# One hybrid encoder layer: the instruction order of the whole program taken from the scheduler's timeline model

## The chip, the cores and the metric

The kernel runs on one core of a Trainium2 chip. The core has five engines that work side by side, each through its own queue in order: TensorE (PE, matrix products and transposes by a product with the identity), VectorE (DVE), ScalarE (ACT), GpSimd (POOL) and SyncE (SP), which here does nothing but issue DMA transfers. An instruction that has to wait for another engine holds up everything behind it on its own engine. The metric is the time of one execution on the device in microseconds (us); less is better.

## The reference

One layer is applied with the same weights to two sequences, 1024 tokens (`x_prompt`) and 256 tokens (`x_sample`), 1280 rows of width 1024 in all, in float32. Cut to what matters:

```python
h = rmsnorm(x); p = h @ w_in                      # one projection, columns shared out
# group A: gated DeltaNet, 4 heads of 128, both directions
qkv = silu(conv5(p[qkv_a])); q, k = l2norm(q), l2norm(k)
#   chunked delta rule per direction: a triangular solve in each chunk, then a scan over the chunks
#   v_new = u - w @ S;  o = q_dec @ S + A @ v_new;  S = S * exp(g) + k_end^T @ v_new
o_a = rmsnorm_head(o_forward + o_backward) * silu(z)
# group B: attention, 4 query heads and 2 key/value heads of 128, RMS-normalised, rotary positions
o_b = softmax(q k^T / sqrt(128)) v
x = x + rmsnorm(concat(o_a, o_b) @ w_out)
x = x + rmsnorm(square(relu(rmsnorm(x) @ w_up)) @ w_down)   # width 4096
```

## The kernel before, in words

Products that need more than one pass's precision are made of three float32r products: each operand is split into a high part (a cast on ACT, L79) and a low part (a subtraction on DVE or POOL, L80), and hi·hi, hi·lo and lo·hi are summed in one PSUM tile. The helper `split` has therefore one pair of lines for almost every stage, and the tile's name tells which one is meant.

The program has these stages. The times behind them are where their instructions stand in the profile of before.

- Rows are loaded, normalised and transposed (`x_proc`), and the `z` columns are projected (`nat_z`): 0 to 95 us.
- The mixed stage, 95 to 536 us. Its pieces are Python generators: `gdn_qk` and `gdn_v` project one head's columns (`proj_T`, matmuls L367 to L369 into `pt`, copied by ACT at L370), run the convolution (`conv_proj`: ACT L440, three DVE steps L443, POOL L444, ACT L445, DVE L446) and hand the result back to PE, which transposes it (`kt` L459, `qt` L473, `vt` L502). `gdn_e`, `gdn_sub` and `gdn_lev` make the decay matrices (`pe` L516 and L522, `pk` L528, `C` L531) and the triangular inverse; `att_proj` projects and rotates the attention heads (`prk` L423). A string written out by hand, `ORDER`, says in which order the generators are stepped. There are 12 convolutions, so 12 such hand-overs from DVE back to PE.
- The scan and attention, 536 to 791 us. `step` (L795 to L842) does one chunk of one head and both directions: products `p` on PE (L798, L800), `r` on DVE (L805), `p` on PE (L810), `vt` on ACT (L813), `p` on PE (L817, L826), then the next state on DVE (L823). The eight chunks of the prompt follow one another, four heads side by side. All calls of `step` are recorded ahead of the attention groups' second half (`att_PV`); scores (`att_S`: `ps_s` L712 to L714, maximum L715 on DVE, exponential L721 on ACT, scaling L727 on POOL) are asked for some 15 tiles ahead (`LA`).
- Output projection and norms (`out_prep`, `out_mm`, `out_norm`, `to_M`): 762 to 938 us.
- The MLP's first product (`up_w`, `up_mm` L1145 to L1147, `up_post`), in a scheme with seven products in place of eight: 906 to 1333 us; its second product (`down_prep`, `prod` L1283 to L1285, sums into `acc` on DVE): 1333 to 1672 us; a last slice with the final norm: 1672 to 1739 us. `down_prep` loads its rows from DRAM (`fr`, L1251) where the first product had put them, and casts them on ACT (L1265).

What sets the order of instructions: Python only records them, in program order, with their tiles. When the `tile.TileContext` of `kernel` closes (L1490), its scheduler plays the recorded program through a model of the machine, in model time. Whenever an engine of the model can take an instruction, it gets, of those whose inputs and tile buffers are there by model time, the one recorded earliest. The order in which each engine got its instructions is the order of its queue on the chip, for SP's DMA issues too, and the choice of buffer among a tag's `bufs` falls in the same play. Then semaphores are put in. So program order is a rank and not the order itself: an instruction recorded later passes one that isn't ready in model time. On the chip, an engine can no longer pass anything.

The default model of the machine and the timeline model differ in how they price instructions, transfers and an engine's queue. Both are part of the library. The kernel's own code, its products, tiles, buffer counts and `ORDER` are the same under either.

## Time and profile before

| | |
|---|---|
| median of 3 runs | 1739.7 us (1735.0 to 1739.98) |
| profiled execution | 1741.06 us, of which 1739.3 us from the first instruction to the last |
| mean granted TensorE clock | 0.981 |
| DMA | 252.68 MB, mean 145 GB/s |

A page of the profile lists the busy time of each engine, then the span in 40 slices of 43.5 us, then groups of instructions. "Busy" on PE counts a matmul from start to its modelled end, and neighbours overlap: in a full stream, matmuls of 512 columns are recorded at 0.39 us each but start 0.23 us apart. "Idle before" is the time an engine stood still just before an instruction, and the name behind it is the engine, tile and line whose end let it go on.

### The profile page before, as it was taken

What the parts mean: (1) busy time and instruction counts of PE and PEld (TensorE: products, weight loads), DVE (VectorE), ACT (ScalarE), POOL (GpSimd) and SP (SyncE); (2) the same over time, 40 slices, a digit from 0 to 9 for tenths busy, and PEclk for the clock granted to TensorE, in tenths of its full rate; (3) what the DMA queues carried; (4) which work ended last, traced back from release to release, by engine and by line L of the source; (5) the groups of instructions that cost most, each with busy time, mean ns of one, the idle gap of its engine ahead of it and who ended that gap; (6) DMA issues with size and microseconds to landing.
All of it is one profiled execution on the core that took longest, in us unless ns stands there. A gap on an engine that the chain in (4) does not pass through costs nothing. (4 is left out here: it accounts for less than half of the span.)

```text
span 1739.3 us, 27944 instructions
## 1 busy us (share of the span) xinstructions
PE 1626.4 (94%) x9799; PEld 1387.8 (80%) x9799; DVE 1267.9 (73%) x2549; ACT 854.6 (49%) x1937; POOL 735.8 (42%) x658
## 2 busy tenths in 40 slices
PE   6999898898997999889988999999989999999997
PEld 5777776777775888668878999999888888888885
DVE  7546798996744778885759954545787978888777
ACT  5236566554345767674446644544465333333422
POOL 3212231321113334440102555554636777788763
PEclk9999999999998999999999999999999999999999
DMA  6113334445447866244333543444556544444234
GB/s 208 70 42 109 97 108 129 137 133 154 133 143 231 273 203 194 79 161 166 104 127 127 178 147 125 151 135 134 187 193 220 154 140 146 132 143 142 86 115 155
DMA packets 208779, 252.68 MB, mean 145 GB/s; under 512 B 35073, under 2 KB 163391, under 8 KB 208639
## 3 DMA queue, kind: packets, MB, share of 16 engines
q1 hardware_dynamic: 208495, 250.77, 45.9%
q8 instruction: 77, 1.26, 0.3%
q14 instruction: 63, 0.52, 0.1%
q0 software_dynamic: 144, 0.13, 0.0%
HBM read 159.75 MB, written 91.10 MB: 144 GB/s over the span
## 5 line engine op out<-in xcount | busy, mean ns | idle before, releaser
L1146 PE MATMUL pd<-mh,ulo 128*128 128x320 f32 x892 | 279.6, 314 | 12.9 <-DVE ulo L80 12.8
L1145 PE MATMUL pd<-mh,uhi 128*128 128x320 f32 x892 | 276.6, 311 | 5.5 <-ACT uhi L79 5.5
L1147 PE MATMUL pd<-ml,uhi 128*128 128x320 f32 x892 | 276.9, 311 | 0.0
L1289 DVE TENSOR_TENSOR acc<-acc,pd 128x512 f32<-128x512 f32 x330 | 206.7, 678 | 44.1 <-PE pd L1285 44.1
L1283 PE MATMUL pd<-dhi,fhi 128*128 128x512 f32 x490 | 192.2, 392 | 1.0 <-DVE acc L1291 1.0
L1284 PE MATMUL pd<-dl,fhi 128*128 128x512 f32 x490 | 192.3, 393 | 0.0
L1285 PE MATMUL pd<-dhi,flo 128*128 128x512 f32 x490 | 191.9, 392 | 0.0
L1146 PEld LDWEIGHTS pd<-mh,ulo 128*128 128x128 f32 x892 | 169.1, 190 | 17.8 <-DVE ulo L80 17.8
L367 PE MATMUL pt<-h_hi,whi 128*128 128x512 f32 (+1 forms) x480 | 178.5, 372 | 0.0
L369 PE MATMUL pt<-h_hi,wlo 128*128 128x512 f32 (+1 forms) x480 | 178.4, 372 | 0.0
L368 PE MATMUL pt<-h_lo,whi 128*128 128x512 f32 (+1 forms) x480 | 178.4, 372 | 0.0
L1145 PEld LDWEIGHTS pd<-mh,uhi 128*128 128x128 f32 x892 | 168.9, 190 | 7.0 <-ACT uhi L79 7.0
L1147 PEld LDWEIGHTS pd<-ml,uhi 128*128 128x128 f32 x892 | 169.0, 190 | 0.0
L1265 ACT CAST fhi<-fr 128x1280 fp32r<-128x1280 f32 x49 | 62.1, 1267 | 212.6 <-PE pd L1284 116.2
L80 POOL TENSOR_TENSOR dl<-dw,dhi 128x1024 fp32r<-128x1024 f32 x49 | 129.0, 2633 | 43.4 <-ACT dhi L79 42.8
L1190 POOL TENSOR_TENSOR s<-u,u 128x320 f32<-128x320 f32 x32 | 34.3, 1071 | 207.6 <-ACT u L1155 140.7
L727 POOL TENSOR_TENSOR P<-P,sm 128x512 f32<-128x512 f32 (+1 forms) x72 | 73.5, 1040 | 95.3 <-DVE sm L725 39.0
L1283 PEld LDWEIGHTS pd<-dhi,fhi 128*128 128x128 f32 x490 | 92.0, 188 | 22.4 <-DVE acc L1291 1.4
L1285 PEld LDWEIGHTS pd<-dhi,flo 128*128 128x128 f32 x490 | 92.0, 188 | 20.7
L1284 PEld LDWEIGHTS pd<-dl,fhi 128*128 128x128 f32 x490 | 92.0, 188 | 20.3
L80 DVE TENSOR_TENSOR ulo<-us,uhi 128x512 fp32r<-128x512 f32 x88 | 76.3, 869 | 43.4 <-ACT uhi L79 42.5
L367 PEld LDWEIGHTS pt<-h_hi,whi 128*128 128x128 f32 x480 | 92.7, 193 | 13.5
(358 smaller groups left out, 4091.0 us busy)
## 6 DMA issues: line engine op xcount, KB each, us to landing
fr<-r_d SPq DMA_DIRECT2D x49, 640.0 KB, 4.3
vis<-vis_d SPq DMA_DIRECT2D x64, 384.0 KB, 4.2
uraw<-in_w_up SPq DMA_DIRECT2D x22, 1024.0 KB, 5.4
r_d<-s SPq DMA_DIRECT2D x128, 160.0 KB, 1.8
r_d<-u SPq DMA_DIRECT2D x96, 160.0 KB, 2.1
dw<-in_w_down SPq DMA_DIRECT2D x28, 512.0 KB, 4.9
wraw<-in_w_in SPq DMA_DIRECT2D x48, 256.0 KB, 3.7
x<-in_x_prompt SPq DMA_DIRECT2D x16, 512.0 KB, 3.4
```

What stands on the lines that cost most here:

```text
L80: (V if leng is None else leng).tensor_tensor(lo, src, f32(hi), ALU.subtract)
L367: T.matmul(pm[:, :n], lhsT=whi, rhs=h_hi[:, k, t0:t0 + n], start=(k == 0), stop=False)
L368: T.matmul(pm[:, :n], lhsT=whi, rhs=h_lo[:, k, t0:t0 + n], start=False, stop=False)
L369: T.matmul(pm[:, :n], lhsT=wlo, rhs=h_hi[:, k, t0:t0 + n], start=False, stop=(k == KD - 1))
L727: G.tensor_tensor(x[:, :kw], x[:, :kw], sm[:, 0:1].to_broadcast([128, kw]), ALU.mult)
L1145: T.matmul(pm, lhsT=w[0][:, k], rhs=mh[b, i][:, k], start=(k == 0), stop=False)
L1146: T.matmul(pm, lhsT=w[1][:, k], rhs=mh[b, i][:, k], start=False, stop=False)
L1147: T.matmul(pm, lhsT=w[0][:, k], rhs=ml[b, i][:, k], start=False, stop=(k == 3))
L1283: T.matmul(pm, lhsT=r[0][:, k, tk], rhs=w[0][:, k], start=(k == 0), stop=False)
L1284: T.matmul(pm, lhsT=r[0][:, k, tk], rhs=w[1][:, k], start=False, stop=False)
L1285: T.matmul(pm, lhsT=r[1][:, k, tk], rhs=w[0][:, k], start=False, stop=(k == Q - 1))
L1289: V.tensor_tensor(half(t, d), half(t, d), pm, ALU.add)
```

## The change

One argument of the context is added; nothing else in the file differs. The play at the close of the context uses the timeline model for the whole program, so the order of every engine's queue, the DMA issues on SP's queue and the buffers chosen can differ. The instructions themselves, their number, shapes and engines stay.

```diff
-    with tile.TileContext(nc) as tc, ExitStack() as ctx:
+    with tile.TileContext(nc, schedule_with_timeline_sim=True) as tc, ExitStack() as ctx:
         build(ctx, tc, I, O)
```

## The prediction

> **What bounds the kernel now.** I read the page's busy times first, then its slices, then a table of busy time by stage, then the waits of PE.
>
> ```profile
> PE 1626.4 (94%) x9799; PEld 1387.8 (80%) x9799; DVE 1267.9 (73%) x2549; ACT 854.6 (49%) x1937; POOL 735.8 (42%) x658
> ...
> PEclk9999999999998999999999999999999999999999
> ```
>
> PE is the bound by a wide margin: 1626.4 of 1739.3 us. An order of instructions takes no work away, so what it can win is PE's idle time, 112.9 us, and what it can lose is more of it. The stages say where that idle time lies (start and end of each stretch; its length; then for each engine busy us and count; granted clock, DMA share, GB/s):
>
> ```profile
> 0.00:95.00 95.00, 80.61 (x380) 61.45 (x381) 56.27 (x154) 35.61 (x65) 25.73 (x32) 0.98 0.40 130
> 95.00:217.00 122.00, 110.25 (x562) 90.17 (x560) 76.33 (x162) 66.32 (x188) 26.15 (x35) 0.96 0.31 86
> 217.00:391.00 174.00, 157.35 (x1306) 125.53 (x1305) 160.86 (x350) 106.66 (x282) 48.94 (x117) 0.98 0.47 126
> 391.00:536.00 145.00, 127.50 (x1152) 102.78 (x1151) 86.71 (x239) 56.31 (x178) 24.84 (x48) 0.93 0.50 147
> 536.00:741.00 205.00, 191.36 (x1225) 159.79 (x1224) 162.85 (x503) 141.54 (x430) 85.74 (x108) 0.99 0.61 197
> 741.00:791.00 50.00, 45.69 (x222) 33.71 (x223) 39.17 (x74) 34.51 (x71) 17.53 (x16) 0.97 0.43 148
> 791.00:906.00 115.00, 113.32 (x549) 94.47 (x548) 70.12 (x146) 49.78 (x112) 7.86 (x6) 1.00 0.40 135
> 906.00:1000.00 94.00, 83.48 (x534) 79.02 (x533) 91.46 (x143) 61.65 (x118) 35.42 (x24) 0.98 0.47 152
> 1000.00:1218.00 218.00, 218.00 (x1490) 218.00 (x1489) 109.67 (x187) 108.40 (x221) 113.40 (x108) 1.00 0.42 138
> 1218.00:1348.00 130.00, 119.08 (x746) 113.57 (x746) 100.30 (x141) 69.52 (x133) 72.62 (x51) 0.97 0.61 200
> 1348.00:1672.00 324.00, 324.00 (x1410) 264.44 (x1409) 269.07 (x371) 106.87 (x97) 245.55 (x93) 1.00 0.44 136
> 1672.00:1739.30 67.30, 55.75 (x241) 44.85 (x239) 45.04 (x85) 17.43 (x50) 32.06 (x26) 0.94 0.39 127
> ```
>
> Length less PE's busy time gives, stage by stage, 14.4, 11.8, 16.7, 17.5, 13.6, 4.3, 1.7, 10.5, 0, 10.9, 0 and 11.6 us. The reader is to see three things. From 1000 to 1218 and from 1348 to 1672 us, 542 us in all, PE is busy all the time: no order can be better there. In the mixed stage (95 to 536 us) PE loses 45.9 us. From 217 to 391 us (160.9 of 174) and from 906 to 1000 us (91.5 of 94) DVE is as full as PE, so there an order can only say which of the two waits.
>
> **What cannot be won.** The first matmul waits for the first rows, and after the last one the final norm must still run:
>
> ```profile
> 9.93 1.33 PE L171 MATMUL xt<-ident,xn 128*128 128x128 f32 x5 [9.93 <-DVE xn L184]
> ...
> 1727.35 0.40 PE L1454 MATMUL pd<-lwt,lrow 128*128 128x512 f32 x1
> ```
>
> 9.93 at the start and 1739.30 − 1727.75 = 11.55 at the end are chains of dependent work. 112.9 − 9.9 − 11.6 = 91.4 us is the most that an order could win.
>
> **The change part by part.** It removes and adds no instruction. It moves any of them, SP's DMA issues included, within what the dependences allow. The trace of before doesn't show the new order, so its cost has to be bounded from both sides. In the two full stretches I cost it at nothing: PE has work in hand there all the time, and DVE (109.7 of 218, 269.1 of 324) and POOL (113.4, 245.6) still have room behind it. That cover would go if a DMA load or a weight split were issued a whole step later; nothing in the rows says so. The same holds for 791 to 906 us.
>
> The mixed stage is where the order is dense. Its PE waits:
>
> ```profile
> PE pe L516 <- DVE C L531: 7.6, 6, 2.5
> PE vt L502 <- DVE vT L446: 7.2, 3, 2.6
> PE ps_s L712 <- ACT q_hi L79: 6.1, 1, 6.1
> PE prk L423 <- DVE araw L426: 4.5, 2, 3.1
> PE qt L473 <- DVE qk L446: 3.6, 2, 2.2
> PE pk L528 <- DVE prod L560: 2.3, 1, 2.3
> PE kt L459 <- DVE qk L446: 1.8, 1, 1.8
> ```
>
> (total us, times, longest.) A convolution ends on DVE at L446, and PE's transposes follow. There are 12 such hand-overs, and PE stands before 6 of them: (7.2 + 3.6 + 1.8) / 6 = 2.1 us each. At the other six, the result is there before PE reaches the transposes: the default order has slack there. One such wait, on PE and on DVE:
>
> ```profile
> 276.76 0.40 PE L369 MATMUL pt<-h_hi,wlo 128*128 128x512 f32 x1
> 276.99 0.40 PE L367 MATMUL pt<-h_hi,whi 128*128 128x512 f32 x1
> 280.04 0.66 PE L502 MATMUL vt<-ident,vT 128*128 128x128 f32 x4 [2.65 <-DVE vT L446]
> ...
> 280.80 0.63 PE L369 MATMUL pt<-h_hi,wlo 128*128 128x512 f32 x1
> 281.23 0.63 PE L367 MATMUL pt<-h_hi,whi 128*128 128x512 f32 x1
> ```
> ```profile
> 273.15 2.36 DVE L88 TENSOR_SCALAR xq<-ssq 128x20 f32<-128x20 f32 x1 [0.94 <-ACT gj L376]
> 275.54 0.18 DVE L89 TENSOR_SCALAR ngh<-xq 128x20 f32<-128x20 f32 x1
> ...
> 278.49 1.49 DVE L446 SCALAR_TENSOR_TENSOR vT<-vT,cy 128x1282 f32<-128x1282 f32 x1
> ```
> ```profile
> 272.38 2.97 POOL L444 TENSOR_TENSOR cy<-cy,vT 128x1282 f32<-128x1282 f32 x1 [8.76 <-DVE cy L443]
> ```
>
> The queue of PE holds the transposes in the middle of a projection whose other matmuls could have run; it can't pass them on the chip. They were late because a DVE instruction of 20 elements took 2.36 us where its neighbour of the same size took 0.18: it ended (275.51) with POOL's large one (275.35). Afterwards matmuls start 0.43 us apart, not 0.23.
>
> My step is this. An order dealt from a finer account of time sets each transpose where its input is due, and no later; lateness that the account doesn't see, like the 2.2 us above, then meets PE at all 12 hand-overs and not at 6. The added waits are 6 × 2.1 = 12.6 us. The slow matmuls after a wait add to that: the half-speed spell begins at or before 280.80 and is over by 284.85, when the 0.39 us records come back:
>
> ```profile
> 284.85 0.39 PE L369 MATMUL pt<-h_hi,wlo 128*128 128x512 f32 x1
> 285.08 0.40 PE L367 MATMUL pt<-h_hi,whi 128*128 128x512 f32 x1
> ```
>
> Taken as some 3.7 us, that is 3.7 × (1 − 0.23/0.43) = 1.7 us lost, an estimate. The mean clock of this stretch is 0.98 and not lower, so I charge it to half of the six waits: 5.1 us. The bounds: zero, if the added hand-overs keep their slack; and 12 × 2.6 + 12 × 1.7 = 52 us, if all 12 are hit once more by the longest wait. I take 17.7, nearest to the rows of the mean wait.
>
> [...]
>
> All other stages at zero, the sum against the profiled execution is 1741.06 + 17.7 = 1758.8. That execution lies 1.4 us above the median of before, and its span 1.8 below itself; against the median I forecast **1757 us**.
>
> **The rivals.**
>
> *Faster: the waits go.* If the timeline model is closer to the chip where it counts, PE's transposes are set behind work that really is ready. The seven rows above sum to 33.1 us, the attention's start (6.1) is a change of stage and stays; half of the other 27.0 is 13.5. From 1218 to 1348 us PE's idle 10.9 has a similar cause, an engine's queue held up by its first instruction:
>
> ```profile
> ACT fhi L1265 <- DMA fr<-r_d: 11.4, 3, 5.1
> ...
> PE pd L1146 <- DVE ulo L80: 7.5, 8, 2.6
> ```
>
> ACT stands before a cast whose rows are still on their way, while the high part of PE's next weights (L79), on which `ulo` hangs, waits behind it. Half of it is 5.5. With three half-speed spells fewer (5.1) that makes 24.1: 1716 us. For it speaks that so many waits are of the kind that a better-dealt queue avoids; against it, that DVE is full in half of the mixed stage.
>
> *Much slower: the scan loses its precedence.* The scan's chunks follow one another; each needs three visits to PE, one to DVE, one to ACT, and now finds the engines at once because it is recorded ahead of the attention. If the timeline model's engines take a queue of ready work ahead of time, a scan instruction comes in behind that. The scan's last work and the attention's:
>
> ```profile
> L856 DVE SCALAR_TENSOR_TENSOR zt<-oa,ro,zt x40: 333/343/1128, 609.7 to 740.0; 128x128 f32<-128x128 f32 x40
> ...
> L741 PE MATMUL po<-p_hi,v_lo x72: 278/394/485, 562.0 to 790.9; 128*128 128x512 f32 x64, 128*128 128x256 f32 x8
> ...
> L721 ACT ACTIVATE P<-ps_s,mx,rsa 128x512 f32<-128x512 f32 x50 | 38.7, 781 | 12.1 <-DVE mx L718 12.1
> L715 DVE TENSOR_REDUCE mx<-ps_s 128x1 f32<-128x512 f32 x52 | 35.2, 684 | 8.1 <-PE ps_s L714 7.6
> ```
>
> The scan has 790.9 − 740.0 = 51 us in hand. One attention job ahead of it at each visit costs 0.78 + 0.68 + 3 × 0.23 = 2.16 us a chunk, 17.2 over eight chunks. From three jobs deep on (52 us) the slack is gone; six deep give 104 − 51 = 53 us, and with the 17.7 above about 1810 us. For it: such a delay hits every chunk. Against it: nothing in the trace of before shows the depth.
>
> *No difference.* The waits come from late results and not from the order, or the order hardly changes: within 5 us, 1740. [...]
>
> **How the numbers follow.** Forecast (slower, some 8 to 50 us) 0.35; scan delayed (1810) 0.17; faster (1716) 0.31; no difference 0.17. About 0.3% (5 us) is what a measurement of this kernel tells from no change. So slower 0.52, faster 0.31, same 0.17. The likeliest case's own range is 1748 to 1790, from the bounds of its step. For 8 in 10 the range reaches from 1710, which leaves out the third of the fast case in which more than the priced waits go, to 1830, which leaves out a third of the scan's case.
>
> **What would show it.** Right: PE's idle time in the mixed stage goes from 45.9 to some 60 us, with more `kt`, `qt` and `vt` rows among PE's waits, more slices below full clock, and the two full stretches unchanged in length (218 and 324 us for the same counts). The scan's case: the last `oa` work later than the last `po` matmul, and a longer stretch between 536 and 906 us. The fast case: fewer PE waits on DVE before 536 us, and the `fhi` row gone from the waits of ACT. The forecast would be wrong if the full stretches lengthen, say because a POOL or DMA step was put late, or if PE's matmuls themselves take longer.

## The result and the profile after

| | before | after |
|---|---|---|
| median of 4 runs | 1739.84 us (1735.0 to 1743.97) | 1796.57 us (1795.58 to 1804.92) |
| profiled execution, its span | 1741.06, 1739.3 | 1804.92, 1803.2 |
| mean granted TensorE clock | 0.981 | 0.952 |

After stands to before as 1.0338, with a 95% interval of 1.0297 to 1.0378: 57 us slower by the medians. The prediction had the direction and, with 1710 to 1830, the range; its forecast of 1757 was 40 us short. The profiled execution of after is the slowest of its four, 8.4 us above the median; what is read from it below is tested by the experiments.

The page of after, its busy times and its clock:

```profile
PE 1637.7 (91%) x9799; PEld 1415.5 (79%) x9799; DVE 1268.6 (70%) x2549; ACT 858.3 (48%) x1937; POOL 733.2 (41%) x658
...
PEclk9999999998888999886999999999999899999999
```

The instructions are the same in number and, on DVE, ACT and POOL, in busy time. PE is busy 11 us longer, at a lower granted clock (0.952 and not 0.981), and the rest of the 64 us is idle time. A slice is 45.1 us here. The clock's row dips in slices 10 to 13 (406 to 586 us), 17 to 19 (721 to 857 us) and 32 (1398 to 1443 us). Two tables of stretches, before and then after, cut at the first attention score, the scan's end, the first transpose of the out-projection and the first matmul of the up-projection (start and end; length; busy us and count of PE, PEld, DVE, ACT, POOL; clock; DMA share; GB/s):

```profile
95.00:536.00 441.00, 395.09 (x3016) 318.47 (x3015) 323.90 (x749) 229.29 (x645) 99.92 (x199) 0.96 0.44 122
536.00:740.00 204.00, 191.16 (x1225) 159.79 (x1224) 161.85 (x500) 141.18 (x430) 85.74 (x108) 0.99 0.61 197
740.00:762.00 22.00, 17.75 (x76) 12.32 (x76) 17.19 (x35) 18.32 (x37) 9.22 (x8) 0.92 0.73 269
762.00:909.00 147.00, 143.73 (x711) 117.82 (x710) 95.47 (x195) 68.82 (x153) 16.17 (x14) 1.00 0.36 118
```
```profile
95.00:540.00 445.00, 398.08 (x3044) 329.37 (x3042) 330.52 (x753) 228.83 (x646) 94.24 (x199) 0.93 0.42 119
540.00:818.00 278.00, 234.79 (x1410) 200.29 (x1408) 188.18 (x564) 169.51 (x490) 99.60 (x124) 0.91 0.49 159
818.00:836.00 18.00, 0.00 (x0) 0.00 (x0) 9.99 (x11) 8.36 (x8) 0.00 (x0) 0.50 0.82 321
836.00:964.70 128.70, 126.26 (x601) 104.69 (x601) 74.61 (x156) 54.39 (x121) 8.45 (x6) 0.98 0.33 111
```

The mixed stage, where the prediction put its loss, idles 46.9 us after 45.9. PE's waits in it are others, though. The longest of after (total us, times, longest):

```profile
PE pe L516 <- DVE C L531: 13.1, 6, 8.3
PE pk L528 <- DVE C L531: 7.8, 4, 4.1
PE pt L367 <- ACT cp L370: 4.2, 2, 3.9
```

None of the 16 rows of this view names L446: the three rows of before that do (7.2, 3.6 and 1.8 us, six waits) are gone.

From the first score to the up-projection PE's idle time goes from 12.8 + 4.3 + 3.3 = 20.4 to 43.2 + 18.0 + 2.4 = 63.6 us, and its busy time from 352.6 to 361.1: 51.7 us in one stage. Cuts inside it show where (after):

```profile
640.00:740.00 100.00, 95.61 (x624) 82.82 (x624) 75.85 (x219) 68.23 (x186) 38.43 (x46) 1.00 0.40 128
740.00:811.00 71.00, 45.39 (x240) 38.51 (x238) 34.01 (x142) 28.18 (x104) 11.88 (x28) 0.81 0.51 171
811.00:836.00 25.00, 0.00 (x0) 0.00 (x0) 13.95 (x31) 10.74 (x18) 0.29 (x1) 0.50 0.59 231
```

Until 740 us PE is about as full as before (95.6 of 100 us). Then it is left with a third of the scan and nothing beside it, and at last with nothing at all. The groups by line say the same (shortest, median and longest ns; first and last start). `vt`, once in each step of the scan, before and after; then, of after, the last attention product:

```profile
L813 ACT ACTIVATE vt<-p,sca x80: 348/367/397, 541.6 to 727.8; 128x128 f32<-128x128 f32 x80
```
```profile
L813 ACT ACTIVATE vt<-p,sca x80: 347/366/452, 552.7 to 808.6; 128x128 f32<-128x128 f32 x80
...
L741 PE MATMUL po<-p_hi,v_lo x72: 278/394/403, 569.3 to 733.6; 128*128 128x512 f32 x64, 128*128 128x256 f32 x8
```

80 records are 40 steps of two directions. The pace of the scan falls from (727.8 − 541.6) / 40 = 4.65 to (808.6 − 552.7) / 40 = 6.40 us a step, while attention's last product comes 57 us earlier (733.6 against 790.9). Before, 44 of the 72 products stand ahead of the scan's last `vt` and 28 behind it; after, all 72 do. A stretch of the timeline of after shows how a step is made longer (start, us, engine, line):

```profile
660.79 0.63 ACT L813 ACTIVATE vt<-p,sca 128x128 f32<-128x128 f32 x2
...
661.41 0.39 PE L740 MATMUL po<-p_lo,v_hi 128*128 128x512 f32 x1
...
661.63 0.39 PE L741 MATMUL po<-p_hi,v_lo 128*128 128x512 f32 x1
...
661.86 0.60 PE L735 MATMUL ptr<-ident,P 128*128 128x128 f32 x4
...
662.22 0.36 PE L712 MATMUL ps_s<-k_hi,q_hi 128*128 128x256 f32 x1
...
662.66 0.61 PE L817 MATMUL p<-vt,vis 128*128 128x128 f32 x4
```

`vt` is there at 661.42. The scan's next product stands in PE's queue behind two attention products, four transposes and three score matmuls, all of them ready, and starts 1.24 us later with PE never idle. No row of waits shows this: PE waits for nothing, the scan waits for PE. Averaged over the 144 products that read a `vt`, the delay from the end of their step's second `vt` to their start is 0.88 us before and 1.73 after; over the 64 that read an `r`, from its end, 0.55 and 1.35.

What the scan's end is worth is seen in the queue behind it: first SP's transfers, then rows of all engines.

```profile
820.68 3.79 SPq L877 DMA_DIRECT2D wo_raw<-in_w_out  x8
```
```profile
816.36 2.19 DVE L856 SCALAR_TENSOR_TENSOR zt<-oa,ro,zt 128x128 f32<-128x128 f32 x8
...
834.00 1.04 ACT L79 CAST wo_hi<-wo_raw 128x1024 fp32r<-128x1024 f32 x1 [0.96 <-DMA wo_raw<-in_w_out]
836.05 1.09 PE L897 MATMUL otr<-ident,og 128*128 128x128 f32 x4 [26.10 <-DMA og<-og_d]
```

The out-projection needs the scan's result back from DRAM. Its weights are asked for when `zt` is done, too: 818.6 to 836.1 us is a chain of transfers and casts. Before, the same chain ran from 740 to 762 us, but PE had 17.75 us of work there, from the rest of attention.

The second place is the change from up to down. First of before (DVE, then PE), then POOL, DVE and PE of after:

```profile
1343.48 6.07 DVE L1291 COPY acc<-pd 128x512 f32<-128x512 f32 x10 [6.88 <-DMA r_d<-s]
```
```profile
1344.83 0.50 PE L1283 MATMUL pd<-dhi,fhi 128*128 128x512 f32 x1 [1.00 <-DVE acc L1291]
```
```profile
1389.87 3.59 POOL L1237 TENSOR_TENSOR dw<-dw 128x1024 f32<-128x1024 f32 x1 [6.45 <-DMA dw<-in_w_down]
1393.42 0.86 POOL L1190 TENSOR_TENSOR s<-u,u 128x320 f32<-128x320 f32 x1
1394.25 0.87 POOL L1192 TENSOR_TENSOR s<-u,u 128x320 f32<-128x320 f32 x1
1395.08 2.34 POOL L1238 TENSOR_TENSOR dw<-dw 128x1024 f32<-128x1024 f32 x1
1397.38 0.85 POOL L1191 TENSOR_TENSOR s<-s,u 128x320 f32<-128x320 f32 x1
1398.20 2.87 POOL L1267 TENSOR_TENSOR flo<-fr,fhi 128x1280 fp32r<-128x1280 f32 x1
1401.03 2.33 POOL L80 TENSOR_TENSOR dl<-dw,dhi 128x1024 fp32r<-128x1024 f32 x1
1403.33 2.33 POOL L1240 TENSOR_TENSOR dw<-dw 128x1024 f32<-128x1024 f32 x1
1405.62 0.85 POOL L1201 TENSOR_TENSOR s<-s,u 128x320 f32<-128x320 f32 x1
```
```profile
1408.54 6.07 DVE L1291 COPY acc<-pd 128x512 f32<-128x512 f32 x10 [17.34 <-DMA r_d<-s]
```
```profile
1409.88 0.80 PE L1283 MATMUL pd<-dhi,fhi 128*128 128x512 f32 x1 [14.34 <-DVE acc L1291]
```

The first copy into `acc` waits in both kernels for the transfer that takes the last sums `s` away (DVE's rows name it). After, those sums stand in POOL's queue between five preparing steps of the down-projection (3.59 + 2.34 + 2.87 + 2.33 + 2.33 us), the first of which itself waits 6.45 us for a transfer of weights. PE's next product needs the PSUM tile that this copy frees, and waits 14.3 us, 13 more than before.

### The profile page after: what moved, and what is told of

Same layout as the page of the kernel before. It is cut to its first block, busy times and chain, and to the rows that moved or that the text cites. A ratio compares the mean times of both kernels' runs of the same rounds, so it can differ in the third digit from the quotient of the medians.

```text
span 1803.2 us, 28033 instructions
## 1 busy us (share of the span) xinstructions
PE 1637.7 (91%) x9799; PEld 1415.5 (79%) x9799; DVE 1268.6 (70%) x2549; ACT 858.3 (48%) x1937; POOL 733.2 (41%) x658
## 5 line engine op out<-in xcount | busy, mean ns | idle before, releaser
L1145 PE MATMUL pd<-mh,uhi 128*128 128x320 f32 x892 | 277.2, 312 | 1.4 <-ACT uhi L79 1.0
L1283 PE MATMUL pd<-dhi,fhi 128*128 128x512 f32 x490 | 193.5, 395 | 14.3 <-DVE acc L1291 14.3
L1145 PEld LDWEIGHTS pd<-mh,uhi 128*128 128x128 f32 x892 | 169.4, 190 | 3.3 <-ACT uhi L79 3.0
L80 POOL TENSOR_TENSOR dl<-dw,dhi 128x1024 fp32r<-128x1024 f32 x49 | 134.6, 2747 | 51.4 <-ACT dhi L79 51.2
L1283 PEld LDWEIGHTS pd<-dhi,fhi 128*128 128x128 f32 x490 | 92.6, 189 | 35.8 <-DVE acc L1291 14.8
L369 PEld LDWEIGHTS pt<-h_hi,wlo 128*128 128x128 f32 x480 | 92.4, 193 | 14.7 <-DVE wlo L80 0.5
```

What stands on the lines that cost most here:

```text
L80: (V if leng is None else leng).tensor_tensor(lo, src, f32(hi), ALU.subtract)
L369: T.matmul(pm[:, :n], lhsT=wlo, rhs=h_hi[:, k, t0:t0 + n], start=False, stop=(k == KD - 1))
L1145: T.matmul(pm, lhsT=w[0][:, k], rhs=mh[b, i][:, k], start=(k == 0), stop=False)
L1283: T.matmul(pm, lhsT=r[0][:, k, tk], rhs=w[0][:, k], start=(k == 0), stop=False)
```

## The experiments

For every kernel the table cuts the span of its profiled execution at the first matmul, the first score (L712), the first up product with split weights (L1145 reading `uhi`; twelve products with `w` come some us earlier) and the start of the last down product (L1283). "Pace" is that of the scan as above. Each median stands against runs of the kernel before on the same chip (1737.6 to 1739.8 us).

| kernel | median us | ratio, 95% interval | first matmul | to first score | score to up | up to last down | rest | pace |
|---|---|---|---|---|---|---|---|---|
| before | 1739.84 | | 9.9 | 525.7 | 373.6 | 762.1 | 67.9 | 4.65 |
| after | 1796.57 | 1.0297 to 1.0378 | 14.1 | 525.9 | 424.7 | 774.3 | 64.2 | 6.40 |
| hold | 1802.26 | 1.0329 to 1.0399 | 14.3 | 520.5 | 431.5 | 770.4 | 64.2 | 5.59 |
| others_depth1 | 1799.35 | 1.0308 to 1.0380 | 15.0 | 537.5 | 416.3 | 768.1 | 64.2 | 6.16 |
| pe_depth1 | 2193.38 | 1.2571 to 1.2667 | 9.4 | 768.5 | 555.4 | 790.1 | 68.6 | 5.64 |
| pe_depth2 | 1732.86 | 0.9943 to 0.9975 | 13.7 | 501.8 | 389.2 | 761.0 | 64.2 | 5.59 |
| pe_depth4 | 1717.97 | 0.9874 to 0.9916 | 9.1 | 500.1 | 384.7 | 761.5 | 64.2 | 5.58 |
| pe_depth8 | 1738.15 | 0.9977 to 1.0010 | 13.2 | 496.4 | 399.0 | 759.6 | 64.2 | 5.90 |
| pe_depth16 | 1760.50 | 1.0111 to 1.0151 | 13.3 | 509.4 | 410.1 | 761.8 | 64.4 | 6.18 |
| pe_order_back | 1771.70 | 1.0169 to 1.0239 | 9.4 | 522.0 | 402.4 | 769.2 | 64.2 | 5.05 |
| pe_order_put_in | 1804.99 | 1.0362 to 1.0404 | 14.7 | 518.7 | 441.0 | 763.1 | 68.0 | 6.83 |
| pool_order_back | 1789.09 | 1.0257 to 1.0313 | 9.1 | 520.4 | 423.9 | 764.4 | 64.5 | 6.37 |
| pe_and_pool_back | 1762.97 | 1.0114 to 1.0158 | 9.3 | 524.7 | 400.7 | 761.8 | 64.2 | 5.01 |
| four_orders_back | 1751.83 | 1.0053 to 1.0104 | 9.0 | 525.1 | 381.8 | 772.2 | 64.2 | 4.70 |
| four_orders_to_end | 1740.08 | 1.0008 to 1.0042 | 13.9 | 520.4 | 381.3 | 757.7 | 67.9 | 4.70 |
| depth4_stage_before | 1709.47 | 0.9813 to 0.9864 | 9.4 | 498.2 | 375.0 | 760.7 | 64.2 | 4.72 |

From before to after the five pieces change by +4.2, +0.2, +51.1, +12.2 and −3.7: 64 us. The first matmul comes at 9 or at 14 us in kernels whose order begins alike (after 14.1, pool_order_back 9.1), so the +4.2 is taken as chance of the execution.

### Is it the attention products, or the depth of the model's queues?

**hold** ties each attention product on PE behind a chunk of the scan, so that 38 of 72 and not all stand ahead of its end; all else is left to the timeline model.

```diff
-            att_PV(vs_[kv], t0, n, c, pend[i], po)
+            with tc.issue_after(behind[0, (0, 0, 0, 1, 1, 2, 2, 2, 3, 3, 3, 4, 4, 4, 5, 5, 6, 6, 6, 7)[min(npv // 2, 19)]].ins):
+                att_PV(vs_[kv], t0, n, c, pend[i], po)
```

> Timeline model as in the change, with one edit: on PE each of the 72 attention products with V is queued behind a given chunk of the scan, at about the pace of before (38 of 72 products stand ahead of the scan's last product in PE's queue; before 44, in the change 72). Theory A (the scan loses its precedence on PE to attention work, is then alone on the engines, and its late end also puts off the loads of w_out): the scan ends by some 745 us, the 26 us gap of PE before otr L897 shrinks to a few us, and 40 to 50 us of the 57 come back: 1745 to 1757 us. Theory B (the loss is spread over stalls of all stages, the scan's late end is just a symptom): 10 us or less come back: 1787 us or more.

Measured: 1802 us, nothing recovered. The pace came back by half (5.59), and the held products no longer filled PE beside the scan: from the first score to the up-projection PE idles 58.4 us, where it idled 63.6 in the change, and is busy 12 us longer than there. The idle time only moved. Cover at the end alone is not the cure.

The other three change a setting of the library's timeline model, its queue depth: the number of instructions that a model engine may take into its queue while the engine itself is still busy. The values that the expectations name are numbers of the model and no measurement; how many instructions a queue of the chip holds, no run here shows.

```diff
+    held = TRN2Spec.ENG_ISSUE_QUEUE_DEPTH
+    TRN2Spec.ENG_ISSUE_QUEUE_DEPTH = {e: 2 if e.name == "PE" else n for e, n in held.items()}
     with tile.TileContext(nc, schedule_with_timeline_sim=True) as tc, ExitStack() as ctx:
         build(ctx, tc, I, O)
+    TRN2Spec.ENG_ISSUE_QUEUE_DEPTH = held
```

**pe_depth1** (1 for PE), **others_depth1** (1 for all but PE) and **pe_depth2** (2 for PE):

> Timeline model, but its model of PE takes only one instruction ahead instead of 35; the other engines' queues stay at 12. Theory A1 (PE of the model takes ready low-ranking work ahead, so that high-ranking work comes in behind it): the order goes back towards program order (16 of 72 attention products ahead of the scan's last), the scan ends before 740 us, time 1730 to 1765 us. Theory A2 (the other prices of the timeline model make the order, not the depth of PE's queue): 1785 us or more.

> Timeline model with PE's queue left at 35 and all other engines' queues at one. Theory A1 (PE's queue alone matters): the order of scan and attention stays as in the change (72 of 72 ahead), time 1785 to 1810 us. Rival (the queues of DVE and ACT delay the scan's hand-overs as well): 20 us or more come back, 1777 us or less.

> Timeline model with two instructions ahead on PE, others at 12: 66 of 72 attention products ahead of the scan's eighth chunk's start and all 72 ahead of its last product; in the change, 72 stand ahead from the sixth chunk on. Theory A1: between one ahead and 35 ahead, 1755 to 1780 us, with a shorter stretch of the scan alone. If the time is that of one ahead, the loss isn't set by how far the attention runs ahead.

The depth of the other engines makes no difference in the total (1799), though in its profile the mixed stage is 12 us longer than after's and the scan's stage 8 us shorter. PE's does: at 2 the 57 us turn into a gain of 7, better than I had expected. At 1 the kernel takes 2193 us, against my expectation. Its first score comes at 778 us and only 16 of 72 products stand ahead of the scan's end: the order goes wrong in every stage but the last, and the run says nothing on the scan.

### Is order the whole of it, and whose?

In the next six kernels queue orders are written out by hand, for the timeline model (or, in pe_order_put_in, for the default one): each instruction of an engine in one part of the program is chained behind the one that the other kernel's queue has ahead of it. The chain only orders; it adds no semaphore.

```diff
+        for step in zlib.decompress(base64.b85decode(text)).decode().split(","):
+            at += int(step)
+            if prev is not None:
+                tc.add_manual_dep(mine[at], prev.name, mybir.DependencyInfo(
+                    mybir.DependencyClass.NoSync, mybir.DependencyReason.DATA), reason="pin")
+            prev = mine[at]
```

> The timeline model, but TensorE's own queue order from the first attention score to the first matmul of the up-projection is that of the kernel before, written out by hand; VectorE, ScalarE, GpSimd and SyncE keep what the timeline model gives them. Theory (the order of TensorE's queue is the loss: each visit of the scan stands behind ready attention work): nearly all of the 52 us of this stage come back, 1745 to 1755 us; the scan's chunk-head step falls from 6.4 to under 5.0 us. Rival (the scan's casts and sums on VectorE and ScalarE stand behind attention work in their own queues): at most 20 us come back, 1777 to 1797 us, and the step stays above 5.6 us.

> The reverse: the default model, but TensorE's queue order in that stage (first attention score to first up matmul) is that of the changed kernel. Theory (TensorE's order is the loss): 1740 + 45 to 52 = 1785 to 1792 us, scan pace about 6.4 us per step and all 72 PV products done ahead of the scan's end. Rival (the orders of the other engines): under 20 us are lost, 1740 to 1760 us.

Put into the kernel before, the changed order of PE alone costs 67 us, more than the change itself and than I had expected. Taken out of the changed kernel, it gives back 25 of 57, between my two cases: the step falls to 5.05 us and not under 5.0. So PE's order is enough to make the loss, but putting it right isn't enough to undo it. The queues of DVE, ACT and POOL were dealt in the same play, in which attention ran ahead; that they go on holding the scan up is tested by four_orders_back below.

> The timeline model, but GpSimd's queue order from the up-projection on is that of the kernel before; the other engines keep what the timeline model gives them. Theory for the 12 us between the up- and the down-projection (the last sums L1190, L1191 and L1201 stand in GpSimd's queue behind five preparing operations of the down-projection, one of which waits for a DMA, and the accumulators reuse the memory that these sums release): the 14.3 us wait of TensorE for L1291 falls to 1 to 4 us, 1781 to 1788 us. Rival (the wait comes from TensorE's own order, down products placed ahead of the last up products): the wait stays above 10 us, 1793 to 1800 us.

GpSimd's order alone gives 7.5 us: the piece from up to down falls by 9.9, and PE's wait is halved:

```profile
1388.82 0.80 PE L1283 MATMUL pd<-dhi,fhi 128*128 128x512 f32 x1 [6.59 <-DVE acc L1291]
```

The reading of POOL's queue was right, the size was not: 6.6 us are left where I expected 1 to 4. In this kernel's trace L1237 still stands ahead of the last sums, after a wait of 5.48 us for its weights' transfer, and L1238 stands among them; whether that holds the rest was not tested.

> Both pieces of order of the kernel before at once (TensorE's in the stage of scan, attention and out-projection, GpSimd's from the up-projection on), everything else from the timeline model. Theory (these two orders are the whole loss): 1797 - 50 - 12 = 1735 to 1745 us. Rival (a further loss elsewhere that they only uncover): above 1755 us.

Both together give 1763 us, not 1740; the two gains add (25 and then 9), and what is missing is in the same stage (400.7 against 373.6).

> As pe_order_back, but the queue orders of VectorE, ScalarE and GpSimd in the stage from the first attention score to the first up matmul are those of the kernel before as well; SyncE's, and everything outside the stage, come from the timeline model. Giving back TensorE's order alone returned 25 us of 57, and putting the changed order of TensorE alone into the kernel before cost 67. Theory (the loss of the stage is order in the queues and nothing else; TensorE's and the others' are each enough to slow the scan): the stage from the first score to the first up matmul falls from 425 to 373 us as before, 1740 to 1752 us. Rival (the rest of the stage's loss comes in from outside: DMA order on SyncE, or operands that the stage before leaves late): at most a few us better than pe_order_back, 1762 to 1775 us.

> The four queue orders of the kernel before from the first attention score to the end of the program, so that the timeline model's order is left in the first stage alone (embedding, norm and input projections, about 95 to 540 us). My prediction put 17.7 us of loss on that stage. As predicted: 1740 + 18 = 1755 to 1760 us. Rival (the profiles of before and after, where the first score starts at 536 and 540 us): 1738 to 1746 us.

With all four queues of the stage as before, it falls to 381.8 us and the median to 1752: 45 us back, 20 more than with PE's queue alone. With the four queues as before up to the end, the median is 1740.1. That is 12 us more, and what is left of the 57 is 2.4 us by the medians and 4.3 by the ratio (1.0025, 1.0008 to 1.0042), and not the 17.7 that I had put on the mixed stage. Its profile shows where they are: the mixed stage itself is not longer (520.4), but the scan's first `vt` comes 13 us behind the first score and not 6.

```profile
L813 ACT ACTIVATE vt<-p,sca x80: 347/367/412, 547.3 to 735.1; 128x128 f32<-128x128 f32 x80
```

(of four_orders_back, whose first score starts at 534.1 us; four_orders_to_end has 547 as well.)

### A dose or a step, and is there a better order?

> The timeline model with TensorE's queue at 4 instructions in place of 35 (the other engines at 1, which by others_depth1 changes nothing). Theory (loss grows with the number of ready attention matmuls that the model lets stand ahead of a scan step: 4.65 us a step before, 5.6 at depth 2, 6.4 at 35): between the two, 1740 to 1765 us. Rival (the depth only has to be over 1 for the model to overlap matmuls, and deeper is no worse until a scan's visit is missed altogether): as pe_depth2, 1728 to 1738 us.

> The timeline model with TensorE's queue at 8 instructions (the other engines at 1). Depth 2 gave 1732.9 us, depth 4 1718.0, depth 35 about 1798. Theory (a dose: each further instruction that may stand in the queue is one more piece of ready attention ahead of a scan step): linear between 4 and 35 it would be 1718 + 4/31 x 80 = 1728 us, so 1722 to 1745, with 64 to 70 of the 72 PV products done ahead of the scan's end only where the scan is slow. Rival (the loss sets in at once when a whole PV or score group fits in the queue, three or more matmuls of 0.2 us each ahead of one scan step): above 1760 us.

> As pe_depth8 with 16. Dose: 1718 + 12/31 x 80 = 1749 us, so 1735 to 1770. Rival (a step): as the change, above 1785 us; or, if the loss needs nearly the whole queue, below 1730 us.

The other engines' depth is 1 in these three. Depths 2, 4, 8, 16 and the library's own of PE's queue in the model give 1732.9, 1718.0, 1738.2, 1760.5 and some 1797 us: from 4 on a dose, steeper at its beginning than a straight line, and no step: 8 and 16 lie in the dose's ranges. With the other engines at 1 throughout (others_depth1 has the library's own for PE), depths 4, 8, 16 and the library's own give 384.7, 399.0, 410.1 and 416.3 us for the scan's stage and a pace of 5.58, 5.90, 6.18 and 6.16. The delay from an `r` to its product, averaged as above, is 1.17, 1.38, 1.41 and 1.47 us (0.83 at depth 2, 0.55 before). So the delay at each step grows with the depth. How many attention products go first does not: at 2, 4, 8 and 16 already 72, 71, 72 and 72 of the 72 start ahead of the scan's last `vt`, where I had expected 64 to 70 at 8. Two limits remain. Between the profiles of pe_depth16 and others_depth1 only 6 of 42 us are the scan's stage, and 28 the mixed stage (537.5 after 509.4). And the depth isn't all of it: at 2 and 4 the pace is 5.6 and not the 4.65 of before.

Depth 4 is the best and lies outside both of my cases; it beats the kernel before by 1.1% (0.9895, 0.9874 to 0.9916). Its gain isn't in the scan, which is slower than before, but ahead of it:

```profile
L712 PE MATMUL ps_s<-k_hi,q_hi x72: 280/473/792, 509.2 to 712.5; 128*128 128x512 f32 x64, 128*128 128x256 f32 x8
```
```profile
L712 PE MATMUL ps_s<-k_hi,q_hi x72: 278/474/796, 535.6 to 770.3; 128*128 128x512 f32 x64, 128*128 128x256 f32 x8
```

The first score starts at 509.2 us (pe_depth4) in place of 535.6 (before). That suggested putting the two best pieces together, **depth4_stage_before**, the mixed stage by the timeline model at depth 4 and the four queues of the scan's stage as the default model dealt them:

> pe_depth4 with the four queue orders of the kernel before in the stage from the first attention score to the first up matmul. pe_depth4 gained 27 us ahead of the first score (509 against 536 us) and lost 12 in this stage (385 against 373 us). Theory (the two add): 1718 - 12 = 1703 to 1710 us. Rival (the early start of the stage is part of its length: scan operands are not ready, so the order of before waits at its start): 1714 to 1722 us.

1709.5 us, 1.6% faster than before (0.9839, 0.9813 to 0.9864): the gains add, and this is the fastest order found.

## Why the prediction was right and wrong

*What bounds the kernel.* Right: the work is the same, and the whole difference is PE's idle time and 11 us more of its busy time, at a granted clock of 0.952 and not 0.981.

*The mixed stage, +17.7 (6 × 2.1 and three half-speed spells).* Wrong. From the first matmul to the first score it takes 525.9 us after 525.7, and four_orders_to_end bounds all that the stage does to the rest at 2 to 4 us. The step that failed is "lateness meets PE at all 12 hand-overs and not at 6": PE waited at none of them. In the trace of after, PE's next transpose (L459, L473 or L502) starts 4.2 us behind the end of L446 in the median and up to 8.9, against 0.13 in the median and up to 2.25 before. The timeline model did not set the transposes where their input is due; it left other work in front of them, as it did in the scan. That much the faster rival had right, but other waits, above all those on `C`, took the place of these. The depths from 2 to 16 show that the stage could even win 16 to 29 us. With PE's queue short in the model, the order has gains of the size of the faster rival (24.1); with the library's own depth, they are given away.

*The full stretches at nothing.* This held. The up-projection takes 423 us in both, and the last 1400 products of the down-projection 322.2 us in both. PE has no idle time from 1412 to 1736 us of after, as from 1348 to 1672 before:

```profile
1412.00:1736.00 324.00, 324.00 (x1402) 264.20 (x1402) 266.36 (x370) 107.41 (x97) 243.78 (x88) 0.99 0.42 131
```

*All other stages at zero.* The last piece won 3.7 us (64.2 for 67.9), in nearly every order of the timeline model. The change from up to down, just ahead of the second full stretch (1218 to 1348 us of before), lost 12.2 us, of which POOL's order alone explains 9.9. The prediction had named such a cause, a step of POOL put late, but as a danger to the full stretches, and said that nothing in the rows spoke for it. What follows is much larger, and it made the miss. Scan, attention and out-projection cost 51.1 us in the profile and 45 by four_orders_back. The second rival (1810 us, chance 0.17) had the mechanism, a queue of ready work ahead of each visit of the scan, and pe_depth2 to pe_depth16 show it as a dose. Its signs came true, too: the scan's last work lies behind attention's (818 and 734 us), and the stage is longer. It should have been the forecast's largest term. That the forecast had the direction right is luck, since the stage that it named lost nothing. Two of its numbers were off, in opposite ways. Its delay of 104 us was too large: the scan ends 278.2 us after the first score in place of 204.4, 74 us later. Its slack of 51 us was not slack. Attention did not stay behind the scan to cover it, it was what delayed the scan, and so it was used up by 733.6 us. The delay cost 51 of its 74 us, and not 74 − 51 = 23.

*The half-speed spells.* In the mixed stage the clock did fall, from 0.96 to 0.93 (95 to 540 us of after) or 0.94 (from the first matmul to the first score), but it cost PE nothing that can be seen. From the first matmul to the first score PE is busy for 475.3 us before and 474.8 after, with 3393 matmuls in both. (The 3.0 us more in the tables from 95 us on are 28 matmuls more in that stretch, since the first matmul comes 4 us later.) Outside that stage, such spells are seen behind the long waits. After the wait of 14.3 us, from the timeline of PE:

```profile
1410.47 0.63 PE L1284 MATMUL pd<-dl,fhi 128*128 128x512 f32 x1
1410.90 0.63 PE L1285 MATMUL pd<-dhi,flo 128*128 128x512 f32 x1
...
1415.16 0.58 PE L1283 MATMUL pd<-dhi,fhi 128*128 128x512 f32 x1
1415.58 0.40 PE L1284 MATMUL pd<-dl,fhi 128*128 128x512 f32 x1
1415.82 0.39 PE L1285 MATMUL pd<-dhi,flo 128*128 128x512 f32 x1
```

Matmuls start 0.43 us apart until 1415.58, 5.7 us after the restart, at a granted clock of 0.50, and 0.23 apart from there, at 1.00 (1415.58 to 1425 us). Behind the wait of 26.1 us, the 0.40 us records come back 6.1 us after the restart (836.05 to 842.19, clock 0.51). In the spell that the prediction shows, after a wait of 2.65 us, the 0.39 us records come back after 4.8 us (280.04 to 284.85 of before, clock 0.65). What sets the length of such a spell, no run shows.

*Not settled:* the 6.6 us that PE still waits with POOL's order put right; the 8 us by which the scan's stage is longer in four_orders_back than before; the pace of 5.6 at depths 2 and 4; why a model queue of one instruction spoils every stage but the last.

## What to carry to other kernels

A chain of short dependent steps lives on finding its engine free, so an order that fills an engine's queue with ready work slows the chain without showing a single wait on that engine (here from 4.65 to 6.40 us a step); look at the delay from a result to its use (0.88 and 1.73 us for `vt`), not only at idle time. Work that seems to be slack behind such a chain, here 51 us, is its cover, and the same reordering that delays the chain uses it up. A scheduler's model is worth tuning by stage: at a queue depth of 4 the timeline model wins 26 us in one stage here and loses 11 in the next, and at the library's own depth it wins nothing and loses 51.

## What the runs showed of the hardware that was not expected

In after, the granted clock was lower where PE had gaps: 1.00 over 640 to 740 us, where PE is busy 95.6 of 100 us, 0.81 over 740 to 811 us, where it is busy 45.4 of 71 us, and 0.50 where it does nothing (811 to 836 us). From the first score to the up-projection, the same work took 361.1 us of PE's busy time in place of 352.6, so about a sixth of that stage's loss is longer busy time and not idle time. The lower clock is the likely cause; no run separates the two. The first matmul came at 9 to 10 us in some executions and at 13 to 15 in others, with nothing between. Of two kernels whose difference lies some 900 us later, after and then pool_order_back:

```profile
14.09 1.97 PE L171 MATMUL xt<-ident,xn 128*128 128x128 f32 x8 [14.09 <-DVE xn L184]
```
```profile
9.11 1.97 PE L171 MATMUL xt<-ident,xn 128*128 128x128 f32 x8 [9.11 <-DVE xn L184]
```

Each kernel was profiled in one execution only, so that the start varies from one execution of a kernel to the next, and is part of the spread of its times, is likely but not shown.
